# Squares of the latents summed on GpSimd, the first scale on TensorE, and the residual weighted earlier

## The chip, the cores and the metric

The kernel runs on one core of one Trainium2 chip. The core has four engines that compute: TensorE (PE in the profile, PEld for its weight loads), VectorE (DVE), ScalarE (ACT) and GpSimd (POOL). SyncE (SP) issues most of the transfers; some are issued from GpSimd's queue. Each engine works through its own queue in order. The metric is the time of one execution on the device in microseconds (us), as the median of the runs shown. The profile is one execution that was recorded in full.

## The reference

A trunk of two layers over 1024 tokens of width 1024, in float32. Each layer scales and shifts its input by values that depend on a conditioning vector c, makes one wide projection, runs three groups of attention heads on parts of it, gates, projects back, adds the residual and normalises:

```python
for l in range(DEPTH):                                   # DEPTH = 2
    mod = silu(c) @ w_ada[l] + b_ada[l]                  # adaLN
    shift, scale, gate = split(mod, 3)
    h = x * (1 + scale) + shift
    (p_cq, p_ckv, p_kr, p_qb, p_kb, p_vb, p_qc, p_kc, p_vc,
     p_qi, p_ki, p_wi, p_gate) = split(h @ w_in[l])
    cq, ckv = rms_norm(p_cq, q_norm_g[l]), rms_norm(p_ckv, kv_norm_g[l])   # the latents: 768 and 256 wide
    o_a = mla_attention(...)        # 6 heads from the latents (queries 768, keys and values 256) and rope
    o_b = dilated_attention(...)    # 6 heads, three dilation patterns, ALiBi
    o_c = sparse_attention(...)     # 4 heads; an indexer of 8 heads picks the top 256 keys of each query
    y = concat(o_a, o_b, o_c) * silu(p_gate)
    x = layer_norm(ALPHA * x + (1 + gate) * (y @ w_out[l]), ln_g[l], ln_b[l])
```

`rms_norm` needs, for each token, the mean of the squares over all features of the latent.

## The kernel before

Activations are held transposed: 8 chunks of 128 features (partitions) by 1024 tokens. TensorE multiplies in a reduced format, so every operand is kept as two tiles, a rounded high part (`hi`, by ScalarE's `Copy`) and the low rest (`lo`, by a subtraction on GpSimd or VectorE), and every product is three matmuls. `split_w` (L188) loads a raw weight tile on SP's queue and splits it; `w_chunk` fetches the weights of one chunk of 128 outputs. There are two raw tiles (`WR`) and four split ones (`W`), so two chunks are held and two more are on their way. `project` (L204) makes one chunk in two halves of 512 tokens into two PSUM banks `pj` and hands each half to a function that empties it.

The program is written in the order of the mathematics. A scheduler then sets each engine's order by running the program against its own estimate of every instruction's length: whatever is ready goes where its engine has room. So an instruction can stand in its engine's queue well ahead of, or behind, the code that it is written next to, and the order is fixed before the run. Some orders are set by tables at the top (`FB` and `FC`: how many of the latent and gate projections are used as filling work behind each head).

The stages of a layer that the change touches:

- **The start** (`begin`, L883, first layer only). For each chunk k of features `part_ada` loads two 128x1024 pieces of the adaLN weights (e = 0 for scale, e = 1 for shift), multiplies each with silu(c) in eight VectorE instructions (L913, L915) and sums over the partitions with one matmul against ones (L916); L918 adds the bias into `mod0`. `part_h` loads the chunk of x, applies scale and shift on ScalarE (L927), makes h's high part on ScalarE (L928) and its low part on GpSimd (L929; the last chunk on VectorE). `part_vb` multiplies h's chunk at once into the values of the dilated heads, accumulated for seven token blocks over seven PSUM banks (L899); the eighth block follows behind (`natural`). `LEAD` says how many chunks `part_ada` is ahead of `part_h`.
- **The indexer and the selection** (L387, L464). VectorE adds up the indexer's scores (L436), and VectorE and ScalarE search the threshold of the top 256 by bits (L462, L480). A tie-break on VectorE ends the selection (L520 to L538): a scan, and comparisons whose inputs all lie in SBUF.
- **The latents** (`latent`, L599). Eight chunks, two of ckv (i = 0, 1) and six of cq. Each half is split into `hi` and `lo`, stored to `cq_d`, squared by ScalarE (L609), transposed by TensorE in four 128x128 pieces (L614) so that tokens lie on partitions, and summed over features by VectorE (L617, L620), whose results are added up over the chunks (L621). `norm_r` makes the reciprocal roots.
- **Attention** (`attend`, L296). Scores on TensorE into three banks `S`; VectorE adds bias and takes the maximum (L283, L286, L289), ScalarE exponentiates (L291), VectorE inverts the sum (L292), GpSimd multiplies the weights by it (L293); TensorE transposes (L315, two banks `T`), the weights are split (L318, L319) and multiplied with the values (L327); the two parts of the result are added (L331, L332) and gated on GpSimd (L334).
- **The output projection** (`out_proj`, L792). For each of eight token blocks (`TBO`) TensorE makes two halves of 512 outputs, 24 matmuls each. VectorE multiplies by the gate (L856), adds the residual (L857), takes statistics (L858, L860, L862), GpSimd the reciprocal root (L863); in the last layer VectorE applies the layer norm (L867, L868) and the block is stored. The first layer stores its normalised blocks in `x1_d` without the norm's gain and offset; the second layer loads each of them as residual and GpSimd multiplies and adds them first (L843, L844). The residual's buffers `XR` are one in the first layer and two in the last.

The scratch in SBUF that GpSimd's own transfers use has the default size.

## Time and profile before

| | |
|---|---|
| runs | 1795.9 us median of 3 (1790.45 to 1797.68) |
| profiled execution | 1791.37 us, of which 1789.5 us are the recorded span |
| mean granted clock of TensorE | 0.978 |
| busy, share of the span | PE 93%, PEld 80%, DVE 78%, ACT 57%, POOL 39% |
| data moved by DMA | 178.93 MB, mean 100 GB/s |

A group row names line, engine, operation, output and inputs (buffer numbers left out), shapes and count; behind the bar stand the busy time and the mean of one in ns, and then the engine's idle time just before and what ended it. A row of the timeline begins with start and length in us; `x3` merges three instructions, and the bracket tells idle time before it and what ended it. Matmuls overlap in the pipeline, so their spacing is read from starts, not from lengths. In a stretch row stand its length and then, after the comma, the busy times of PE, PEld, DVE, ACT and POOL with their counts, TensorE's granted clock, the DMA share and GB/s. A row of slices has one digit for each 44.7 us, in tenths. A row of waits has who waited for whom, us in all, times and the longest.

### The profile page before, as it was taken

What the parts mean: (1) busy time and instruction counts of PE and PEld (TensorE: products, weight loads), DVE (VectorE), ACT (ScalarE), POOL (GpSimd) and SP (SyncE); (2) the same over time, 40 slices, a digit from 0 to 9 for tenths busy, and PEclk for the clock granted to TensorE, in tenths of its full rate; (3) what the DMA queues carried; (4) which work ended last, traced back from release to release, by engine and by line L of the source; (5) the groups of instructions that cost most, each with busy time, mean ns of one, the idle gap of its engine ahead of it and who ended that gap; (6) DMA issues with size and microseconds to landing.
All of it is one profiled execution on the core that took longest, in us unless ns stands there. A gap on an engine that the chain in (4) does not pass through costs nothing. (4 is left out here: it accounts for less than half of the span.)

```text
span 1789.5 us, 26735 instructions
## 1 busy us (share of the span) xinstructions
PE 1662.4 (93%) x9080; PEld 1440.0 (80%) x9080; DVE 1396.6 (78%) x3266; ACT 1022.0 (57%) x2010; POOL 697.8 (39%) x625
## 2 busy tenths in 40 slices
PE   4899899999998999989999989999999999998993
PEld 4778688888896888877899978888789788987882
DVE  8889788889588678886763678888948866788589
ACT  3244499895544666674113649998544367767500
POOL 3421134233434355463322113323343345666274
PEclk9899999999999999999999999999999999999997
DMA  9465113233212521222332212242220244122232
GB/s 345 147 220 189 48 55 92 78 119 102 75 36 62 212 92 57 84 68 92 110 130 51 71 59 56 75 142 83 74 92 20 67 171 141 45 76 91 71 106 94
DMA packets 55364, 178.93 MB, mean 100 GB/s; under 512 B 7606, under 2 KB 8630, under 8 KB 54716
## 3 DMA queue, kind: packets, MB, share of 16 engines
q1 hardware_dynamic: 50812, 147.86, 24.7%
q0 software_dynamic: 4416, 29.36, 5.7%
q8 instruction: 72, 1.18, 0.3%
q14 instruction: 64, 0.52, 0.1%
HBM read 129.74 MB, written 34.87 MB: 92 GB/s over the span
## 5 line engine op out<-in xcount | busy, mean ns | idle before, releaser
L199 PE MATMUL pj<-h,w 128*128 128x512 f32 (+1 forms) x3408 | 831.1, 391 | 13.9 <-DVE qk L233 5.4
L199 PEld LDWEIGHTS pj<-h,w 128*128 128x128 f32 x3408 | 632.2, 191 | 131.6 <-issue 12.6
L193 POOL TENSOR_TENSOR w<-wr,w 128x1024 fp32r<-128x1024 f32 (+2 forms) x86 | 192.9, 2244 | 284.4 <-ACT w L192 262.7
L199 PE MATMUL S<-qk,qk 128*128 128x512 f32 (+2 forms) x1104 | 281.9, 360 | 11.0 <-DVE mx L283 4.6
L293 POOL TENSOR_SCALAR pr<-pr,den 128x896 f32<-128x896 f32 (+7 forms) x180 | 139.0, 776 | 257.3 <-DVE den L292 214.0
L318 ACT ACTIVATE pt<-T 128x512 fp32r<-128x512 f32 (+1 forms) x320 | 172.1, 551 | 112.6 <-PE T L315 56.3
L319 DVE TENSOR_TENSOR pt<-T,pt 128x512 fp32r<-128x512 f32 (+1 forms) x320 | 199.6, 633 | 43.1 <-ACT pt L318 38.9
L327 PE MATMUL O<-pt,v 128*128 128x256 f32 (+1 forms) x1280 | 213.0, 286 | 7.3 <-DVE pt L319 4.2
L199 PEld LDWEIGHTS S<-qk,qk 128*128 128x128 f32 x1104 | 185.2, 191 | 36.7 <-DVE mx L283 8.7
L480 ACT ACTIVATE scr<-acc,U 128x768 uint8<-128x768 f32 x186 | 193.2, 1039 | 33.6 <-DVE U L476 18.1
L327 PEld LDWEIGHTS O<-pt,v 128*128 128x128 f32 x1280 | 185.6, 191 | 24.0 <-DVE pt L319 6.8
L334 POOL TENSOR_TENSOR g<-g,osum 64x256 f32<-64x256 f32 x128 | 98.6, 770 | 224.0 <-DVE osum L332 222.3
L291 ACT ACTIVATE pr<-pr,mx 128x384 f32<-128x384 f32 (+7 forms) x188 | 145.6, 775 | 54.7 <-DVE mx L283 36.4
L315 PE MATMUL T<-ident,pr 128*128 128x128 f32 x852 | 144.7, 278 | 9.7 <-POOL pr L293 5.1
L462 DVE TENSOR_SCALAR_CACHE_REDUCE scr<-acc,U 128x384 uint8<-128x384 f32 x186 | 138.4, 744 | 3.8
L192 ACT ACTIVATE w<-wr 128x1024 fp32r<-128x1024 f32 (+2 forms) x86 | 83.8, 976 | 65.0 <-PE pj L199 62.3
L315 PEld LDWEIGHTS T<-ident,pr 128*128 128x128 f32 x852 | 101.4, 141 | 21.0 <-POOL pr L293 6.5
L199 PE MATMUL pj<-w,h 128*128 128x256 f32 (+2 forms) x672 | 107.0, 300 | 1.4 <-DMA h<-cq_d 1.2
L199 PEld LDWEIGHTS pj<-w,h 128*128 128x128 f32 x672 | 91.7, 190 | 6.3 <-DMA h<-cq_d 1.4
L331 ACT ACTIVATE osum<-O 64x256 f32<-64x256 f32 x128 | 48.6, 380 | 58.5 <-PE O L327 55.3
L436 DVE SCALAR_TENSOR_TENSOR acc<-S,wi,acc 128x512 f32<-128x512 f32 (+1 forms) x84 | 56.2, 679 | 30.6 <-ACT S L431 30.3
L332 DVE TENSOR_TENSOR osum<-O,osum 64x256 f32<-64x256 f32 x128 | 53.4, 417 | 26.2 <-ACT osum L331 22.6
(277 smaller groups left out, 2565.2 us busy)
## 6 DMA issues: line engine op xcount, KB each, us to landing
wr<-in_wt_dram SPq DMA_DIRECT2D x62, 512.0 KB, 3.6
cq_d<-rw SPq DMA_DIRECT2D x64, 256.0 KB, 2.0
h<-cq_d POOLq DMA_DIRECT2D x4, 4096.0 KB, 20.2
qk<-qk POOLq DMA_DIRECT2D x48, 256.0 KB, 2.9
pt<-in_w_ada_dram SPq DMA_DIRECT2D x22, 512.0 KB, 4.0
wr<-in_w_out_dram SPq DMA_DIRECT2D x16, 512.0 KB, 3.5
bi<-in_bias_dram SPq DMA_DIRECT2D x14, 512.0 KB, 4.1
bi<-in_w_ada_dram SPq DMA_DIRECT2D x10, 512.0 KB, 4.5
```

The costliest lines, as they stand in the source:

```text
L192: act.activation(hi[:, :n], raw[:, :n], AF.Copy)
L193: (lo_eng or pool).tensor_tensor(lo[:, :n], raw[:, :n], bc(hi[:, :n]), OP.subtract)
L199: pe.matmul(ps, lhsT=l, rhs=r, start=(i == 0), stop=(i == len(items) - 1))
L291: act.activation(p[:, :n], p[:, :n], AF.Exp, bias=m, scale=-1.0, accum_out=den)
L293: (dve if ne[qb] else pool).tensor_scalar(p[:, :n], p[:, :n], den, 0.5, OP.mult, OP.mult)
L315: pe.transpose(t[:, c:c + P], p[j](2 * kp + kk), ident)
L318: act.activation(pt[:, 0, :n], t[:, :n], AF.Copy)
L319: dve.tensor_tensor(pt[:, 1, :n], t[:, :n], bc(pt[:, 0, :n]), OP.subtract)
L327: pe.matmul(o[:, oc], lhsT=vt(kb), rhs=pt[:, e, pc], start=(kb == 0 and e == 0), stop=(kb == 2 * g + 1 and e == 1), skip_group_check=True)
L334: pool.tensor_tensor(yc, yc, s[r0:r0 + 64], OP.mult)
L462: dve.tensor_scalar(scr8[:, :IDX_LEN[b]], scores(b), s, None, op, OP.add, accum_out=dst[:, b:b + 1])
L480: act.activation(scr[:, :IDX_LEN[b]], scores(b), AF.Sign, bias=U[:, b:b + 1].bitcast(F32), accum_out=cnt[:, b:b + 1])
```

## The change

- **Latents.** Two tiles (`RES` for ckv, `LNG` for cq) hold the squares of the first chunk; GpSimd adds the squares of each later chunk to them (24 additions of 128x512 over both layers). Only after the last chunk of each latent are four transposes for each half made, and one reduction: 32 transposes in place of 128, and 8 reductions in place of 32.
- **Start.** The scale (e = 0) is made on TensorE: eight accumulating matmuls with the weight piece as stationary operand and a column of silu(c) as the moving one, in place of eight VectorE instructions and one matmul. The shift stays as it was. The low parts of h and of the value weights are made on VectorE in place of GpSimd. `LEAD` is 1, and `part_h` stands ahead of `part_ada`.
- **Residual.** In the second layer the weighting by gain and offset of the first layer's norm is emitted behind the latent heads 0 to 3, two blocks each (`NRES`): load into `RES`, multiply and add on GpSimd, store to `xw_d`. The output projection loads the weighted block from there, and has `RES` as one more residual buffer in both layers. `LNG` and `LNB` hold the gain and offset; the last layer's are loaded into the same tiles after that.
- The three new tiles (12 KB a partition) are paid for by a smaller scratch for GpSimd's transfers.

```diff
-LEAD = 3
+LEAD = 1
+NRES = ((0,0,0,0,0,0),(2,2,2,2,0,0))
...
+    RES, LNG, LNB = [sb.tile([P, 1024], F32, name=n) for n in ("res", "lng", "lnb")]
+    xw_d = [dr.tile([P, 1024], F32, name=f"xw_d{i}") for i in range(NB)]
...
     def latent(l, i):
-        sums = rk if i < 2 else scq
+        sums, row = (rk, RES) if i < 2 else (scq, LNG)
...
-            hi, lo, sq = RW.next().bitcast(F32R), RW.next().bitcast(F32R), PR.next()
+            hi, lo = RW.next().bitcast(F32R), RW.next().bitcast(F32R)
+            sq = row[:, cols] if i in (0, 2) else PR.next()
...
             act.activation(sq, ps, AF.Square)
...
-            t = ps_t.tile([P, 4, P], F32, name="T")
-            for j in range(4):
-                pe.transpose(t[:, j, :], sq[:, j * P:(j + 1) * P], ident)
-            to = sums[:, half * 4:half * 4 + 4]
-            if i in (0, 2):
-                dve.tensor_reduce(to, t, AX.X, OP.add)
-            else:
-                s4 = small.tile([P, 4], F32, name="s4")
-                dve.tensor_reduce(s4, t, AX.X, OP.add)
-                dve.tensor_tensor(to, to, s4, OP.add)
+            if i not in (0, 2):
+                pool.tensor_tensor(row[:, cols], row[:, cols], sq, OP.add)
+            if i in (1, 7):
+                t = ps_t.tile([P, 4, P], F32, name="T")
+                for j in range(4):
+                    pe.transpose(t[:, j, :], row[:, cols.start + j * P:cols.start + j * P + P], ident)
+                dve.tensor_reduce(sums[:, half * 4:half * 4 + 4], t, AX.X, OP.add)
...
     def mla(l, values):
...
+            for _ in range(NRES[l][h]):
+                residual(rest.pop(0))
+
+    def residual(i):
+
+        if i == 0:
+            sp.dma_start(LNG, a["ln_g"][0].to_broadcast([P, 1024]))
+            sp.dma_start(LNB, a["ln_b"][0].to_broadcast([P, 1024]))
+        tb = TBO[i]
+        sp.dma_start(RES, x1_d[tb])
+        pool.tensor_tensor(RES, RES, LNG, OP.mult)
+        pool.tensor_tensor(RES, RES, LNB, OP.add)
+        sp.dma_start(xw_d[tb], RES)
...
     def out_proj(l):
-        XR = Ring([AC[0]] + ([G.tiles[f]] if last else []))
+        XR = Ring([AC[0], RES] + ([G.tiles[f]] if last else []))
...
-            sp.dma_start(xr, x1_d[tb] if last else a["x"][tb])
-            if last:
-                pool.tensor_tensor(xr, xr, lgb[0], OP.mult)
-                pool.tensor_tensor(xr, xr, lgb[1], OP.add)
+            sp.dma_start(xr, xw_d[tb] if last else a["x"][tb])
...
         def part_ada(k):
...
+                to = o_ps[:, 0, 2 * k + e:2 * k + e + 1]
+                if e == 0:
+                    for c in range(8):
+                        pe.matmul(to, lhsT=w[:, c * P:(c + 1) * P], rhs=cs[:, c:c + 1], start=(c == 0), stop=(c == 7),
+                                  skip_group_check=True)
+                    continue
...
         def part_h(k):
-                hi, lo = split_w(a["wvb"][0, k // 2], 784, ring=QK, raws=raws)
+                hi, lo = split_w(a["wvb"][0, k // 2], 784, ring=QK, lo_eng=dve, raws=raws)
...
-            (dve if k == 7 else pool).tensor_tensor(HA[k][1], x, bc(HA[k][0]), OP.subtract)
+            dve.tensor_tensor(HA[k][1], x, bc(HA[k][0]), OP.subtract)
...
-    nc = bacc.Bacc("TRN2", target_bir_lowering=False, num_devices=1)
+    nc = bacc.Bacc("TRN2", target_bir_lowering=False, num_devices=1, dynamic_dma_scratch_size=4096)
```

The scheduler's order at the three places that matter most. A row has the line in its own file, so the same statement has another number in the changed kernel (L193 is L198 there, L293 is L298, L334 is L339, L617 is L625, L233 is L238).

GpSimd's queue at the program's start, before; `qk` are the value weights' parts, `h` the chunks of h, `w` the weight chunks of the indexer:

```order
L193 TENSOR_TENSOR qk_77<-wr_91,qk_76 128x784
L929 TENSOR_TENSOR h<-v,h 128x1024 x2
L193 TENSOR_TENSOR qk_79<-wr_92,qk_78 128x784
L929 TENSOR_TENSOR h<-v,h 128x1024 x2
L193 TENSOR_TENSOR qk_81<-pt_89,qk_80 128x784
L193 TENSOR_TENSOR qk_83<-pt_90,qk_82 128x784
L929 TENSOR_TENSOR h<-v,h 128x1024 x2
L193 TENSOR_TENSOR w_85<-wr_91,w_84 128x1024
L929 TENSOR_TENSOR h<-v,h 128x1024
L193 TENSOR_TENSOR w_87<-wr_92,w_86 128x1024
```

And now, with the indexer's first instructions behind them:

```order
L198 TENSOR_TENSOR w_85<-wr_91,w_84 128x1024
L198 TENSOR_TENSOR w_87<-wr_92,w_86 128x1024
L410 TENSOR_TENSOR rw_100<-rw_100,pr_93 32x512
L198 TENSOR_TENSOR w_85<-wr_91,w_84 128x1024
L241 DMA qk_76<-qk_76 64x1024
L242 DMA qk_77<-qk_77 64x1024
```

The eleven subtractions of the start have left this queue (for VectorE's); two weight splits stay.

GpSimd's queue in the second layer, in the sparse heads, where VectorE does the selection's tie-break, before:

```order
L334 TENSOR_TENSOR g_8696<-g_8696,osum 64x256
L193 TENSOR_TENSOR w_87<-wr_92,w_86 128x1024
L193 TENSOR_TENSOR w_85<-wr_91,w_84 128x1024
L293 TENSOR_SCALAR bi_8693<-bi_8693,den 128x256
L334 TENSOR_TENSOR g_8696<-g_8696,osum 64x256
L193 TENSOR_TENSOR w_87<-wr_92,w_86 128x1024
L236 DMA qk_80<-qk_80 64x1024
```

And now (`res` is the residual, weighted by `lng` and `lnb`):

```order
L805 TENSOR_TENSOR res<-res,lng 128x1024
L339 TENSOR_TENSOR g_8615<-g_8615,osum 64x256
L806 TENSOR_TENSOR res<-res,lnb 128x1024
L198 TENSOR_TENSOR w_87<-wr_92,w_86 128x1024
L198 TENSOR_TENSOR w_85<-wr_91,w_84 128x1024
L805 TENSOR_TENSOR res<-res,lng 128x1024
L339 TENSOR_TENSOR g_8615<-g_8615,osum 64x256
L806 TENSOR_TENSOR res<-res,lnb 128x1024
L198 TENSOR_TENSOR w_87<-wr_92,w_86 128x1024
L805 TENSOR_TENSOR res<-res,lng 128x1024
L241 DMA qk_80<-qk_80 64x1024
```

The residual's instructions, written behind the latent heads, stand here one whole group of heads earlier, between the splits of the weights. All sixteen stand from just behind the last latent to the end of the tie-break.

VectorE's queue in the first layer where the indexer ends, the first two latents are summed and the first dilated head's projection is emptied from the banks `pj`, before:

```order
L226 TENSOR_TENSOR qk_76<-pj,qk_76 64x512
L441 TENSOR_TENSOR acc<-acc,causb 128x128
L436 SCALAR_TENSOR_TENSOR acc<-S,wi,acc 128x512
L617 TENSOR_REDUCE rk<-T 128x4
L462 TENSOR_SCALAR scr,cnt_124<-acc 128x512
L226 TENSOR_TENSOR qk_76<-pj,qk_76 64x512
L436 SCALAR_TENSOR_TENSOR acc<-S,wi,acc 128x512
L441 TENSOR_TENSOR acc<-acc,causb 128x128
L617 TENSOR_REDUCE rk<-T 128x4
L233 TENSOR_TENSOR qk_78<-pj,qk_77 64x512
L462 TENSOR_SCALAR scr,cnt_124<-acc 128x640
L620 TENSOR_REDUCE s_1548<-T 128x4
```

And now:

```order
L231 TENSOR_TENSOR qk_76<-pj,qk_76 64x512
L446 TENSOR_TENSOR acc<-acc,causb 128x128
L441 SCALAR_TENSOR_TENSOR acc<-S,wi,acc 128x512
L625 TENSOR_REDUCE rk<-T 128x4
L467 TENSOR_SCALAR scr,cnt_127<-acc 128x512
L231 TENSOR_TENSOR qk_76<-pj,qk_76 64x512
L441 SCALAR_TENSOR_TENSOR acc<-S,wi,acc 128x512
L446 TENSOR_TENSOR acc<-acc,causb 128x128
L625 TENSOR_REDUCE rk<-T 128x4
L238 TENSOR_TENSOR qk_78<-pj,qk_77 64x512
L467 TENSOR_SCALAR scr,cnt_127<-acc 128x640
L238 TENSOR_TENSOR qk_78<-pj,qk_77 64x512
```

Ahead of the first instruction that empties the second part of a bank (L233, now L238) stand as many instructions as before, two reductions among them; only the reductions behind it are gone.

More of the change, by code (lines that the diff above doesn't have):

```diff
@@ L758, in query @@
             project(wh, wl, 6, CA, evac)
-        q, y = {}, {}
+        q, y, rest = {}, {}, list(range(NB))
         keys(0)
@@ L821, in out_proj @@
         sp.dma_start(g1, g1_d[l].to_broadcast([P, 1024]))
-        lgb = []
         if last:
-            for t, src in zip([fresh("pt0", F32), fresh("pt1", F32), PR3[2], PR3[1]],
-                              (a["ln_g"][0], a["ln_b"][0], a["ln_g"][1], a["ln_b"][1])):
-                sp.dma_start(t, src.to_broadcast([P, 1024]))
-                lgb.append(t)
+            sp.dma_start(LNG, a["ln_g"][l].to_broadcast([P, 1024]))
+            sp.dma_start(LNB, a["ln_b"][l].to_broadcast([P, 1024]))
         else:
@@ L866, in out_proj @@
                     cols = slice(n * 512, (n + 1) * 512)
-                    dve.scalar_tensor_tensor(r[:, cols], r[:, cols], mv[:, 0:1], lgb[2][:, cols], OP.subtract, OP.mult)
-                    dve.scalar_tensor_tensor(r[:, cols], r[:, cols], rs, lgb[3][:, cols], OP.mult, OP.add)
+                    dve.scalar_tensor_tensor(r[:, cols], r[:, cols], mv[:, 0:1], LNG[:, cols], OP.subtract, OP.mult)
+                    dve.scalar_tensor_tensor(r[:, cols], r[:, cols], rs, LNB[:, cols], OP.mult, OP.add)
                     sp.dma_start(out[tb][:, cols], r[:, cols])
@@ L908, in part_ada @@
                     dve.tensor_scalar(bcol[:, 0, :], bcol[:, 0, :], 1.0, None, OP.add)
-                part = cols[:, (2 * k + e) % 8, :]
+                to = o_ps[:, 0, 2 * k + e:2 * k + e + 1]
[4 more added lines that the diff above has]
+                    continue
+                part = cols[:, k % 8, :]
                 for c in range(8):
@@ L915, in part_ada @@
                         dve.scalar_tensor_tensor(part, wc, cs[:, c:c + 1], part, OP.mult, OP.add)
-                pe.matmul(o_ps[:, 0, 2 * k + e:2 * k + e + 1], lhsT=part, rhs=ones, start=True, stop=True,
-                          skip_group_check=True)
+                pe.matmul(to, lhsT=part, rhs=ones, start=True, stop=True, skip_group_check=True)
             dve.tensor_tensor(mod0[:, :, k], o_ps[:, 0, 2 * k:2 * k + 2], bcol[:, :, k], OP.add)
@@ L928, in part_h @@
             act.activation(HA[k][0], x, AF.Copy)
-            (dve if k == 7 else pool).tensor_tensor(HA[k][1], x, bc(HA[k][0]), OP.subtract)
+            dve.tensor_tensor(HA[k][1], x, bc(HA[k][0]), OP.subtract)
         for k in range(-LEAD, 9):
+            if 0 <= k < 8:
+                part_h(k)
             if 0 <= k + LEAD < 8:
                 part_ada(k + LEAD)
-            if 0 <= k < 8:
-                part_h(k)
             if k > 0:
```

## The prediction, made before the changed kernel was run

> **What bounds the kernel now.** I read the page's busy times and slices first, then the stretches at both ends, then the timeline at the places that the change touches.
>
> ```profile
> span 1789.5 us, 26735 instructions
> PE 1662.4 (93%) x9080; PEld 1440.0 (80%) x9080; DVE 1396.6 (78%) x3266; ACT 1022.0 (57%) x2010; POOL 697.8 (39%) x625
> PE   4899899999998999989999989999999999998993
> 1760.00:1789.50 29.50, 0.60 (x3) 0.18 (x1) 25.76 (x39) 0.00 (x0) 9.44 (x7) 0.57 0.27 98
> ```
>
> TensorE is the bound through the middle: its slices read 8 or 9. It falls off in the first two slices and in the last, where in 29.5 us it works 0.60 (first number) while VectorE works 25.76 (third). So time is to be had from work on TensorE in the middle and from whatever holds TensorE or the output up at the two ends. GpSimd has 61% of the span free.
>
> **The end.** In the second layer's output projection GpSimd weights each residual block (L843, L844) while VectorE finishes blocks. The rows show one such meeting, TensorE's last matmul, the distance of two blocks on TensorE, and the last block's finish, which nothing disturbs.
>
> ```profile
> L843 POOL TENSOR_TENSOR acc<-acc,pt 128x1024 f32<-128x1024 f32 x4 | 10.7, 2680 | 8.2 <-DMA acc<-x_d 8.1 <-DMA pt<-in_ln_g_dram 0.2
> 1730.68 1.52 PE L199 MATMUL pj<-v,h 128*128 128x512 f32 x6
> 1741.56 1.52 PE L199 MATMUL pj<-v,h 128*128 128x512 f32 x6
> 1754.87 1.66 PE L199 MATMUL pj<-v,h 128*128 128x512 f32 x6 [2.26 <-DVE acc L856]
> 1755.11 2.56 POOL L843 TENSOR_TENSOR acc<-acc,pt 128x1024 f32<-128x1024 f32 x1 [2.34 <-DMA acc<-x_d]
> 1755.45 5.58 DVE L868 SCALAR_TENSOR_TENSOR pr<-pr,rs,pr 128x512 f32<-128x512 f32 x2
> 1760.21 0.39 PE L199 MATMUL pj<-rw,h 128*128 128x512 f32 x1
> ...
> 1780.72 0.69 DVE L856 TENSOR_TENSOR pr<-pj,bi 128x512 f32<-128x512 f32 x1
> ...
> 1784.53 1.41 DVE L868 SCALAR_TENSOR_TENSOR pr<-pr,rs,pr 128x512 f32<-128x512 f32 x2
> ```
>
> Two instructions of L868 take 5.58 us beside GpSimd and 1.41 without: VectorE stands while GpSimd runs a two-input instruction. L856, which reads one input from PSUM, is not stretched. TensorE needs 1741.56 - 1730.68 = 10.9 us a block. VectorE alone needs three instructions of 512 columns for the first half of a block (L856 and two more, 0.69 each), then 1780.72 to 1785.94 for the second half and the finish: 2.1 + 5.2 = 7.3 us. So VectorE is late only through the sixteen GpSimd instructions (16 x 2.65 = 42 us), and ends 28.9 us behind the last matmul (1760.6 to 1789.5). The change moves the sixteen away and loads finished blocks; the earlier loads are into three buffers and not late. Then only the last block's finish follows the last matmul: 1780.72 to 1789.5, 8.8 us. Gain 28.9 - 8.8 = 20.1, and the wait of 2.26 before 1754.87 with it: **22.4 us**. Ends: 15 if VectorE still trails by one block of 7.3; not more than 22.4.
>
> **The start.** The h of chunk k needs scale and shift from the adaLN weights (16 loads), made by 128 VectorE instructions, then two of ScalarE and a subtraction on GpSimd.
>
> ```profile
> 24.36 2.44 POOL L929 TENSOR_TENSOR h<-v,h 128x1024 fp32r<-128x1024 f32 x1 [1.18 <-ACT h L928]
> 24.50 2.45 DVE L915 SCALAR_TENSOR_TENSOR g<-pr,cs,g 128x128 f32<-128x128 f32 x1
> 31.83 0.61 PE L916 MATMUL O<-ones,g 128*128 128x1 f32 x4
> 42.14 0.70 PE L899 MATMUL S<-qk,h 128*128 128x392 f32 x3
> 42.28 1.23 ACT L927 ACTIVATE v<-v,mod 128x1024 f32<-128x1024 f32 x1
> 42.67 0.52 PE L899 MATMUL T<-qk,h 128*128 128x392 f32 x2
> 44.16 1.04 ACT L928 ACTIVATE h<-v 128x1024 fp32r<-128x1024 f32 x1
> 54.27 1.18 PE L899 MATMUL S<-qk,h 128*128 128x392 f32 x3
> 55.25 0.86 PE L899 MATMUL T<-qk,h 128*128 128x392 f32 x2
> 78.70 14.24 PE L199 MATMUL pj<-h,w 128*128 128x512 f32 x66
> ...
> 10.00:20.00 10.00, 1.76 (x6) 1.50 (x6) 10.00 (x39) 3.04 (x3) 1.01 (x1) 1.00 1.03 415
> 50.00:60.00 10.00, 6.98 (x28) 6.98 (x29) 9.89 (x28) 3.24 (x3) 6.95 (x3) 0.66 0.10 35
> ```
>
> The last two rows are stretches: VectorE is full (10.00, 9.89), and at 50 to 60 the queues are nearly idle (35 GB/s against 415), so VectorE is the bound there, not the loads. One VectorE instruction of 128x128, 0.34 us by itself, takes 2.45 beside GpSimd. The change takes 64 of the 128 off VectorE; puts 64 matmuls of one column on TensorE, at most 0.61 / 4 = 0.15 each, 9.8 us less the 1.2 of eight that go; and moves the seven subtractions and four weight splits from GpSimd to VectorE, where a 1024-wide one costs about 1.4 (twice L856's 0.69). VectorE then has about 8 x (8 x 0.34 + 1.4) + 4 = 37 us of work where it is now full past 60. The next limits are two. The loads before the last x, about 16 MB at 415 GB/s, are in near 42; the chain behind (1.4 for the scale, 2.3 on ScalarE, 21 matmuls at 0.53 / 3 = 0.18, 24 more for the eighth block) ends at 54. TensorE: first h near 14.5 (loads by 10, a split on ScalarE and VectorE, 2.3 on ScalarE), then 168 x 0.18 = 30, 6/8 of the one-column matmuls 8, the 24 of the eighth block 4.3, about 2 for a slow clock at first (0.33 a matmul at 54.27, against 0.18), 2.6 where chunk 1's shift stands behind chunk 0's matmuls, 2 from the two weight splits that GpSimd keeps: 63.4. The chunk projection that starts at 78.70 starts there: **15 us**, taken between 24 (the loads' end) and 2 (rival below). LEAD 1 shortens the queue of loads ahead of x; it is in these numbers.
>
> **The latents.** Of 128 transposes of squares, 96 go. In the middle of the layer and at the start of selection they look like this:
>
> ```profile
> 403.45 0.60 PE L614 MATMUL T<-ident,pr 128*128 128x128 f32 x4
> 403.81 5.75 PE L199 MATMUL pj<-h,w 128*128 128x512 f32 x24
> ...
> 214.91 0.69 DVE L233 TENSOR_TENSOR qk<-pj,qk 64x512 fp32r<-64x512 f32 x1
> 215.70 10.49 PE L199 MATMUL pj<-h,w 128*128 128x512 f32 x40
> ...
> L620 DVE TENSOR_REDUCE s<-T 128x4 f32<-128x512 f32 x24 | 16.2, 687 | 0.2
> L372 POOL TENSOR_TENSOR h<-g,h 128x512 fp32r<-128x512 f32 x8 | 10.9, 1367 | 34.2 <-ACT h L371 34.2
> ```
>
> Four occupy TensorE from 403.45 to 403.81, 0.09 each. 80 of the 96 stand in such full stretches: 80 x 0.09 = **7.2 us** (0 to 8). The other 16 stand, eight a layer, where TensorE waits anyway: its next projection needs the PSUM bank that L233 empties at 215.6 and starts at 215.70. VectorE's row there keeps as many instructions ahead of that L233, so I count nothing. 24 reductions of 0.69 leave VectorE, at nothing gained, since TensorE is full beside them. 24 additions of 128x512 enter GpSimd, about 1.37 each by L372, 33 us, on an engine that is busy 39% of the time; the sources of the next VectorE instructions are in PSUM, as L856's, so nothing is blocked: 0, at most 10 where an addition stands ahead of a softmax weight. [...]
>
> **The residual, moved.** Emitted in the second layer's attention, its GpSimd instructions stand, in that queue's row, earlier: from the last latents through the dilated heads' end, six of the sixteen among the top-k's tie-break. There VectorE has two-input work from SBUF:
>
> ```profile
> 1382.21 5.29 POOL L193 TENSOR_TENSOR w<-wr,w 128x1024 fp32r<-128x1024 f32 x2 [6.00 <-ACT w L192]
> 1382.48 2.82 DVE L538 SCALAR_TENSOR_TENSOR acc<-scr,bi 128x640 f32<-128x640 uint8 x1
> 1385.56 2.37 DVE L527 TENSOR_SCALAR scr<-acc,thr 128x768 uint8<-128x768 f32 x1
> 1385.69 0.62 PE L199 MATMUL S<-qk,qk 128*128 128x384 f32 x2 [0.70 <-DVE mx L283]
> 1388.40 12.32 PE L199 MATMUL pj<-h,w 128*128 128x512 f32 x46 [2.09 <-DVE v L359]
> 1393.49 0.96 DVE L538 SCALAR_TENSOR_TENSOR acc<-scr,bi 128x768 f32<-128x768 uint8 x1
> 1394.48 0.69 DVE L527 TENSOR_SCALAR scr<-acc,thr 128x896 uint8<-128x896 f32 x1
> PE T L315 <- POOL pr L293: 5.1, 5, 2.0
> wr<-in_wt_dram SPq DMA_DIRECT2D x62, 512.0 KB, 3.6
> ```
>
> Beside L193, L538 takes 2.82 for 0.96 and L527 2.37 for 0.69: 1.8 us a GpSimd instruction, and TensorE waited 0.70 + 2.09 = 2.8 of these 3.6. Six times 1.8 x 0.78 is **8 us lost**. The other ten precede softmax weights (L293), for which TensorE waits 5.1 us in the whole run; I add nothing. Ends: 0 and 30. Sixteen DMAs are added on SP's queue; each store waits for GpSimd, and weight loads stand behind it. Two raw tiles and two split ones put the weights two chunks ahead, and a chunk is 48 matmuls (twice 5.75 us at 403.81): 23 us against a round of 12.5 (below), so I cost that at nothing. The second x buffer in the first layer's output projection: nothing, TensorE is full there.
>
> **Sum.** 1789.5 - 22.4 - 15 - 7.2 + 8 = 1752.9 us of span. The profiled execution took 1791.4, 1.9 more, and the median of three, 1795.9, is 4.5 above it: 1759 us. One per cent of this kernel is 18 us; 0.5%, 9 us, is what a measurement can tell.
>
> **Rivals.**
> - The start hardly gains. At 54.27 the matmuls run at 0.33 instead of 0.18 after a gap. If each of seven chunks leaves TensorE a gap and its first twelve matmuls run so, 12 x 0.15 = 1.8 us is lost on each, 13 in all, and 2 are left of 15: 1772. For it: ScalarE's 2.3 us lie between scale and matmul. Against: in the new order scales of the next chunks mostly stand ahead of a chunk's matmuls. [...]
> - The residual takes back more in the tie-break, 15 to 30 us instead of 8: 1766 to 1781. For it: VectorE there is what TensorE waits for, and reordered attention follows.
> - The end does not empty: VectorE or a late load still holds it, gain 5: 1776. Against: 7.3 us of work a block against 10.9.
> - Slower: the single residual buffer. A load (3.6), two GpSimd instructions (5.3) and a store, taken as long as a load, are a round of 12.5 us, and a GpSimd that waits for the load blocks every softmax weight behind it. It decides from (36.6 + 8 + 9) / 8 = 6.7 us a residual passed on to TensorE; at 8 us each, 1759 - 8 + 64 = 1815. Against: the order leaves two or three instructions between rounds, and TensorE hardly waits for GpSimd now.
>
> **Chances.** Forecast, 1746 to 1772: 0.64; start 0.12; tie-break 0.14; end 0.06; slower 0.04. Range 1742 to 1783: below, the start at its best; above, the tie-break's and the end's cases. Faster than 1787: 0.92; within 0.5%: 0.04 (a poor end and a dear tie-break together); slower: 0.04.
>
> **What would show it.** End: last output about 9 us behind the last matmul, no VectorE instruction above 1.5 us per pair there. Start: the first chunk projection of 48 and more matmuls near 63. Latents: 32 transposes of squares, no gain around the early ones. Residual: VectorE's tie-break instructions above 2 us, more than now, and TensorE idle in 1330 to 1400. I am wrong if TensorE's idle time in the middle grows by over 20 us, or if the last matmul comes no earlier than 1745.

## The result, and the profile after

The changed kernel took 1766.5 us (median of 4 runs, 1765.2 to 1771.7) against 1796.7 (1790.5 to 1797.7): 0.9845 of the time before, interval 0.9815 to 0.9874, 30 us faster. The forecast was 1759 (1742 to 1783), 37 us faster. Timed again on another occasion it came to 0.9868 (0.9844 to 0.9892). So sign and range held. The forecast was a ratio of 0.9794 (1759 to 1795.9); by the two ratios measured, 9 to 13 us of the gain did not come. The page of its profile, with the rows that were read first of the kernel before:

```profile
span 1769.9 us, 26708 instructions
PE 1670.7 (94%) x9096; PEld 1449.3 (82%) x9096; DVE 1344.7 (76%) x3165; ACT 1020.3 (58%) x2010; POOL 696.9 (39%) x638
PE   8999899999998999989999999999999799998998
```

Both ends of TensorE's row are filled now. In the middle a 7 has appeared, at 1372 to 1416 us, where a 9 stood. This profiled execution took 1771.7, the slowest of its four runs, and that of before was one of the fastest of its own: the spans differ by 19.6 us, the medians by 30.

**The end.** The last stretch of the span, TensorE's last matmul, and VectorE's first and last instruction for the last block:

```profile
1761.00:1769.87 8.87, 0.45 (x2) 0.02 (x1) 5.09 (x9) 0.00 (x0) 0.92 (x1) 0.68 0.16 59
1761.06 0.39 PE L204 MATMUL pj<-rw,h 128*128 128x512 f32 x1
1761.48 0.69 DVE L867 TENSOR_TENSOR pr<-pj,bi 128x512 f32<-128x512 f32 x1 [3.29 <-PE pj L204]
1765.30 1.41 DVE L879 SCALAR_TENSOR_TENSOR pr<-pr,rs,lnb 128x512 f32<-128x512 f32 x2
```

The output ends 8.4 us behind the last matmul (1761.45 to 1769.87) instead of 28.9, and VectorE does only nine instructions in it. But the last matmul stands at 1761, where it stood before (1760.6): whatever was won ahead of it was lost again in this execution.

**The start.** Two stretches of 10 us, a group of sixteen of the new one-column matmuls (L924) at each speed, three matmuls at each speed, and the first chunk projection:

```profile
20.00:30.00 10.00, 9.74 (x48) 9.66 (x47) 6.42 (x15) 5.46 (x5) 0.00 (x0) 0.67 1.02 406
30.00:40.00 10.00, 10.00 (x46) 10.00 (x45) 6.07 (x15) 3.05 (x3) 0.00 (x0) 0.65 1.04 386
21.83 2.15 PE L924 MATMUL O<-cs,bi 128*128 128x1 f32 x16 [0.26 <-DVE mod L936]
25.06 1.18 PE L910 MATMUL S<-qk,h 128*128 128x392 f32 x3
28.98 3.41 PE L924 MATMUL O<-cs,g 128*128 128x1 f32 x16
38.85 0.70 PE L910 MATMUL S<-qk,h 128*128 128x392 f32 x3
39.74 1.84 PE L924 MATMUL O<-cs,pr 128*128 128x1 f32 x16
71.79 14.24 PE L204 MATMUL pj<-h,w 128*128 128x512 f32 x66
```

TensorE is full (9.74, 10.00) and VectorE is not (6.42, 6.07): the bound has moved. The granted clock is 0.67 and 0.65; from 23.4 to 37.1 us, 13.65 us in all, it is 0.50 (called half clock from here on). The projection starts at 71.8 instead of 78.7, not at 63.4.

**The tie-break of the second layer.** First its stretch from the first scan to its end in the kernel before:

```profile
1363.58:1417.33 53.75, 49.30 (x293) 43.22 (x292) 52.30 (x79) 17.20 (x33) 19.23 (x13) 0.97 0.17 50
```

Then the changed kernel: the stretch from its last counts to its first scan and the one from there to its end, GpSimd's root of the latents' sum, the residual's first instruction, its first in the tie-break and its last, two VectorE instructions of the tie-break, and TensorE's longest wait:

```profile
1279.53:1347.79 68.26, 65.45 (x382) 57.01 (x381) 39.57 (x110) 30.54 (x64) 45.76 (x35) 1.00 0.39 132
1347.79:1411.48 63.69, 50.26 (x285) 42.86 (x283) 62.43 (x70) 14.83 (x27) 35.19 (x18) 0.92 0.37 122
1292.46 1.68 POOL L646 TENSOR_TENSOR scq<-scq,mhalf 128x8 f32<-128x8 f32 x1
1296.63 2.40 POOL L805 TENSOR_TENSOR res<-res,lng 128x1024 f32<-128x1024 f32 x1 [2.49 <-DMA lng<-in_ln_g_dram]
1351.77 2.39 POOL L805 TENSOR_TENSOR res<-res,lng 128x1024 f32<-128x1024 f32 x1 [3.97 <-DMA res<-x_d]
1376.77 2.62 DVE L532 TENSOR_SCALAR scr<-acc,thr 128x768 uint8<-128x768 f32 x1
1384.95 3.03 DVE L543 SCALAR_TENSOR_TENSOR acc<-scr,bi 128x768 f32<-128x768 uint8 x1
1394.10 7.99 PE L204 MATMUL pj<-h,w 128*128 128x512 f32 x24 [5.91 <-DVE qk L238]
1404.95 2.68 POOL L806 TENSOR_TENSOR res<-res,lnb 128x1024 f32<-128x1024 f32 x1
```

From 1351.77 to the end eight of the residual's sixteen instructions run in the tie-break; the other eight run just ahead of it, from 1296.63. L532 takes 2.62 us for 768 columns, where 896 columns take 0.69 undisturbed, and L543 takes 3.03 for 768 columns, which take 0.96 undisturbed. VectorE is full (62.43 of 63.69). TensorE stands for 13.4 us, where it stood for 4.45 before, and for 2.8 in the stretch ahead: 16.2 in all. The bracket at 1296.63 names what held the residual back until then: the load of the gain into `LNG`, the tile in which the latents' squares were summed until just before.

### The profile page after: what moved, and what is told of

It reads as the page before. It is cut to its first block, busy times and chain, and to the rows that moved or that the text cites. A ratio compares the mean times of both kernels' runs of the same rounds, so it can differ in the third digit from the quotient of the medians.

```text
span 1769.9 us, 26708 instructions
## 1 busy us (share of the span) xinstructions
PE 1670.7 (94%) x9096; PEld 1449.3 (82%) x9096; DVE 1344.7 (76%) x3165; ACT 1020.3 (58%) x2010; POOL 696.9 (39%) x638
## 4 chain that ended last, share of the span: by engine, by line
PE 59%; DVE 21%; ACT 10%; issue 5%; DMA 4%; POOL 1%; SPq 0%; DVEq 0%; ACTq 0%; POOLq 0%
PE pj L204 33%; PE S L204 12%; PE O L332 5%; ACT scr L485 4%; PE T L320 4%; DVE pt L324 2%; DVE scr L467 2%; DVE pr L536 1%; DVE acc L441 1%; ACT pr L296 1%; ACT pt L323 1%; DVE acc L543 1%; DVE g L261 1%; DVE pr L288 1%; PE T L204 1%
## 5 line engine op out<-in xcount | busy, mean ns | idle before, releaser
L198 POOL TENSOR_TENSOR w<-wr,w 128x1024 fp32r<-128x1024 f32 (+2 forms) x86 | 190.7, 2218 | 301.0 <-ACT w L197 290.4
L204 PE MATMUL S<-qk,qk 128*128 128x384 f32 (+2 forms) x1104 | 279.2, 361 | 15.0 <-DVE mx L288 8.4
L204 PEld LDWEIGHTS S<-qk,qk 128*128 128x128 f32 x1104 | 187.6, 192 | 41.8 <-DVE mx L288 10.2
L298 POOL TENSOR_SCALAR pr<-pr,den 128x640 f32<-128x640 f32 (+7 forms) x182 | 138.9, 767 | 205.2 <-DVE den L297 164.9
L296 ACT ACTIVATE pr<-pr,mx 128x128 f32<-128x128 f32 (+7 forms) x192 | 146.4, 763 | 51.0 <-DVE mx L288 35.7
L339 POOL TENSOR_TENSOR g<-g,osum 64x256 f32<-64x256 f32 x128 | 98.9, 773 | 191.7 <-DVE osum L337 179.0
L320 PEld LDWEIGHTS T<-ident,pr 128*128 128x128 f32 x849 | 100.5, 141 | 19.2 <-issue 6.0
```

The costliest lines, as they stand in the source:

```text
L198: (lo_eng or pool).tensor_tensor(lo[:, :n], raw[:, :n], bc(hi[:, :n]), OP.subtract)
L204: pe.matmul(ps, lhsT=l, rhs=r, start=(i == 0), stop=(i == len(items) - 1))
L296: act.activation(p[:, :n], p[:, :n], AF.Exp, bias=m, scale=-1.0, accum_out=den)
L298: (dve if ne[qb] else pool).tensor_scalar(p[:, :n], p[:, :n], den, 0.5, OP.mult, OP.mult)
L320: pe.transpose(t[:, c:c + P], p[j](2 * kp + kk), ident)
L339: pool.tensor_tensor(yc, yc, s[r0:r0 + 64], OP.mult)
```

## The experiments

Ratios are to the kernel before, on the same chip and the same occasion; compare them, not microseconds of different occasions. Where the expectations speak of 52.9, 14.8 or 16.6 us in the tie-break, its stretch is taken from the last counts (1279.53 us in the changed kernel), with all sixteen of the residual's instructions inside; from its first scan on there are eight.

| kernel | median us | ratio | interval |
|---|---|---|---|
| changed | 1766.5; again 1769.2 | 0.9845; 0.9868 | 0.9815 to 0.9874; 0.9844 to 0.9892 |
| latents' part alone | 1790.1 | 0.9979 | 0.9963 to 0.9995 |
| start's part alone | 1784.8 | 0.9951 | 0.9934 to 0.9968 |
| residual's part alone | 1762.7 | 0.9830 | 0.9808 to 0.9853 |
| changed, nothing weighted | 1748.7 | 0.9753 | 0.9727 to 0.9778 |
| changed, residual first | 1754.6 | 0.9791 | 0.9771 to 0.9812 |
| the same, scale half on TensorE | 1747.5 | 0.9754 | 0.9734 to 0.9773 |
| the same, scale on VectorE | 1768.7 | 0.9877 | 0.9854 to 0.9899 |
| the same, scale 128 wide | 1750.8 | 0.9775 | 0.9752 to 0.9799 |
| changed without latents' part | 1751.8 | 0.9777 | 0.9755 to 0.9799 |
| residual first, half and wide | 1752.3 | 0.9777 | 0.9754 to 0.9799 |
| no latents, half and wide | 1758.0 | 0.9811 | 0.9789 to 0.9832 |

The three parts alone sum to 0.0021 + 0.0049 + 0.0170 = 0.0240, that is 43 us, and the residual alone is at least as good as the whole change. The whole is worth 0.0132 to 0.0155: 15 to 19 us are lost where the parts meet. The changed kernel was timed on two of the four occasions, the second time together with the last three kernels of the table. Its ratio differs by 0.0023 (4 us) between the two, so differences from it across occasions are good to some 4 us.

**The latents' part alone** (`latent`'s part of the diff, the new tiles and the smaller scratch).

> The kernel before with the latents' part alone. Forecast's theory: 80 of the 96 transposes that go stand in full stretches of TensorE, 0.09 us each, so 7 us faster than before, 1789 to 1790, and nothing at the early latents. Rival: the new order of the middle gives it back (TensorE's idle time behind 100 us grew from 63.4 to 79.6 us between the two profiles), and the part alone is worth nothing: 1797, within 3 us of before.

4 us faster: between the two. The first layer's tie-break from its first scan, in the kernel before and then in this one, and the wait behind it in this one:

```profile
507.88:562.75 54.87, 49.70 (x287) 43.01 (x286) 53.20 (x84) 18.27 (x36) 20.33 (x13) 0.97 0.16 49
```

```profile
511.47:563.62 52.15, 42.31 (x251) 37.00 (x249) 50.53 (x69) 15.38 (x27) 17.67 (x10) 0.95 0.17 52
564.72 3.02 PE L201 MATMUL S<-qk,qk 128*128 128x512 f32 x8 [6.56 <-DVE mx L285]
```

TensorE is idle for 9.8 us there instead of 5.2. The transposes that went stood nowhere near (the last at 416 us before the change). But the scheduler made another order: VectorE now does 69 instructions in the stretch instead of 84, the last seven of the tie-break in one piece, and the attention that TensorE waits for stands behind them. At the early latents nothing was gained, as forecast: the projection that starts at 215.70 before starts at 220.50 here. This profiled execution has the span of the one before (1789.3 and 1789.5 us); the 4 us are those of the medians.

**The start's part alone** (`begin` and `LEAD`).

> The kernel before with the start's part alone. Forecast: the first chunk projection 15 us earlier, near 63, and 15 us faster, 1782. What the changed kernel's profile says: the projection starts at 71.8 instead of 78.7, 6.9 us, and TensorE has no free time left before it (the one-column matmuls are two records each and hold it some 20 us, a part of it at half clock); then 7 us faster at most, 1790, and 4 us (1793) if the 3 us that are lost again before 210 belong to this part.

9 us faster, more than the 7 read from the changed kernel's profile and less than the 15 forecast. Its projection starts at 73.3 in the profile, 5.4 us earlier, with 17.1 us at half clock on the way, the most of the six profiles that have this start; that execution took 1787.9, three more than the median.

**The residual's part alone** (`residual`, `out_proj`, the new tiles).

> The kernel before with the residual's part alone. Forecast: 22.4 us off the end, 8 back in the tie-break of the second layer, 1782. Read from the changed kernel's profile: 20 off the end, 10 back (TensorE's gaps in the tie-break 14.8 us instead of 4.5), 1786 to 1787. Rival: the tie-break and what follows take all of it, 1797.

30 us faster: all three expectations were wrong, and too low. GpSimd's first and last instruction of the residual, and the second layer's tie-break from its first scan:

```profile
915.04 2.39 POOL L806 TENSOR_TENSOR res<-res,lng 128x1024 f32<-128x1024 f32 x1 [2.33 <-DMA res<-x_d]
999.80 2.41 POOL L807 TENSOR_TENSOR res<-res,lnb 128x1024 f32<-128x1024 f32 x1
1358.93:1412.67 53.74, 49.30 (x293) 43.26 (x292) 52.29 (x79) 17.20 (x33) 19.22 (x13) 0.97 0.17 50
```

Without the latents' part nothing else uses `RES` and `LNG`, and the scheduler puts the sixteen, though they are written behind the latent heads, at 915 to 1002 us, into the indexer. The tie-break is as it was before the change: 53.7 us, TensorE idle for 4.4 (53.75 and 4.45 before).

**Nothing weighted.** `mla` doesn't call `residual`, and the output projection loads `x1_d`; so gain and offset of the first layer are left out of the residual.

> The changed kernel without the weighting of the residual in the second layer's attention (the output projection adds the first layer's block without gain and offset): sixteen GpSimd instructions and sixteen transfers less in the middle, all else the same. If the GpSimd instructions in the tie-break cost 10 us, it is 10 us faster than the changed kernel, 1756, VectorE's tie-break instructions sum to about 43 us instead of 52.9, and TensorE's gaps there fall from 14.8 to about 4.5. If the order of the middle costs it, whatever GpSimd does there, it stays within 3 us of 1766 and the gaps stay.

0.9753: the gain is 16 to 21 us over the changed kernel, more than expected. VectorE's tie-break instructions sum to 40.2 us, and TensorE's gaps in the stretch for which 14.8 and 16.6 are quoted are 7.8. Its profile also has the better start (67, see below), so not all of the difference is the residual's.

**The residual written first.**

```diff
-            for _ in range(NRES[l][h]):
-                residual(rest.pop(0))
...
+        for i in range(NB if l else 0):
+            residual(i)
         jobs = [lambda i=i: latent(l, i) for i in range(8)] + ...
```

> The whole change, with the residual's weighting written ahead of the second layer's latents instead of behind the latent heads. The latents' squares use the same two tiles (RES and LNG), so in the changed kernel the weighting cannot start before the last latent is summed, and then it falls into the tie-break; in the kernel with the residual's part alone it ran at 915 to 1003 us, in the indexer. If that is what the change loses, this one is 17 to 18 us faster than the changed kernel, 1749, as without any weighting (1748.7), with the sixteen instructions near 900 to 1000, the tie-break's sum at 40 to 42 us instead of 52.9 and TensorE's gaps there at 4 to 8 us instead of 16.6. Rival: GpSimd's two-input instructions cost VectorE as much wherever they stand, and it stays within 5 us of 1766.

```profile
912.05 2.38 POOL L803 TENSOR_TENSOR res<-res,lng 128x1024 f32<-128x1024 f32 x1 [2.49 <-DMA res<-x_d]
1277.82:1341.57 63.75, 63.75 (x376) 56.35 (x374) 38.82 (x111) 31.57 (x66) 27.09 (x27) 1.00 0.26 83
1341.57:1391.73 50.16, 42.31 (x273) 38.33 (x272) 48.55 (x69) 13.61 (x25) 12.63 (x9) 0.93 0.15 48
```

Place and tie-break are as expected: the two stretches that in the changed kernel took 68.3 and 63.7 us, with 2.8 and 13.4 of idle on TensorE, take 63.8 and 50.2, with none and 7.85. VectorE's tie-break instructions sum to 40.2 us for 52.9, 12.7 less, which is about 1.6 us for each of the eight GpSimd instructions that lay among them. The time is 0.9791, 10 to 14 us better than the changed kernel's 0.9845 and 0.9868. Against the second of these the rival's 5 us lie outside the interval (8 to 20), against the first they do not (3 to 16); the tie-break's own stretches settle it, with 18 us less in them. Of the 17 expected, some are missing in the median. The same sixteen instructions cost 10 to 14 us more in and ahead of the tie-break than in the indexer.

**Scale half on TensorE** (from the residual-first kernel).

```diff
-                if e == 0:
+                if e == 0 and k % 2 == 0:
...
-                part = cols[:, k % 8, :]
+                part = cols[:, (2 * k + e) % 8, :]
```

> The kernel just above, with the scale on TensorE for the even chunks only and on VectorE for the odd ones. In the changed kernel's start TensorE is what is full (gaps of 3.2 us before the chunk projection at 71.8, one-column matmuls 22.0 us) and VectorE works 51.8 of 71.8 us. If that is the bound, 9 us leave TensorE and 11 enter VectorE, both stay under 63, the projection starts near 64 to 66 and the kernel is 5 to 7 us faster than the one above. Rival: VectorE becomes the bound again, as before (80.1 of 78.7 us), and nothing is gained: within 2 us of the one above.

7 us faster in the medians, as expected, but not in the way expected: the projection starts at 69.95 instead of 71.20, and another 4 us come between there and 250 us. Why was not followed further. (The 51.8 and 80.1 us of the expectation seem to add up instructions' lengths, which overlap; the stretches give VectorE 45.79 of 71.79 us in the changed kernel and 67.86 of 78.70 before.) It has the lowest ratio of the kernels that compute everything, and its interval (0.9734 to 0.9773) lies below both of the changed kernel's, though it overlaps those of others around 0.9775.

**Scale wholly on VectorE** (`if e == 0` never taken, `part` as just above).

> The residual-first kernel with the scale wholly on VectorE as before the change; the low parts on VectorE, LEAD and the order of the start as changed. If VectorE was slow in the start only through the lock by GpSimd's subtractions, 128 instructions of 0.34 us and 14 us of low parts are 57 us, the projection starts at 64 to 70 and the total is that of the residual-first kernel within 3 us or a little better: the first scale on TensorE bought nothing. Rival: the move to TensorE is what gains, and without it the projection starts near 77, 5 to 6 us slower than the residual-first kernel.

The rival. A stretch of its start, one of TensorE's waits, and the projection:

```profile
30.00:40.00 10.00, 8.73 (x50) 8.37 (x50) 10.00 (x30) 3.89 (x4) 2.14 (x1) 1.00 1.01 389
24.89 1.02 PE L908 MATMUL pj<-qk,h 128*128 128x392 f32 x2 [2.71 <-ACT h L944]
76.60 9.06 PE L204 MATMUL pj<-h,w 128*128 128x512 f32 x39
```

VectorE is full (10.00; 9.84 and 9.93 in the stretches beside this one) with GpSimd nearly idle, TensorE waits at the head of chunks, and the projection starts 5.4 us later. The 57 us for VectorE were too few. Of the other 9 us of the 14 by which it is slower, most are lost between 250 and 800 us, where TensorE is idle for 31.3 us against 24.7 in the residual-first kernel. The two kernels do the same work there, in another order; which instruction of it costs the time was not followed.

**Scale 128 columns wide.**

```diff
-                    pe.matmul(to, lhsT=w[:, c * P:(c + 1) * P], rhs=cs[:, c:c + 1], ...
+                    pe.matmul(o_ps[:, 0, x:x + P], lhsT=w[:, c * P:(c + 1) * P],
+                              rhs=cs[:, c:c + 1].to_broadcast([P, P]), ...
```

> The residual-first kernel with the scale's matmuls 128 columns wide (the same column repeated) instead of one; a record of 128x128 takes 0.11 us like one of a single column at full clock, so the work is the same. The changed kernel's clock was 0.5 from 23.3 to 36.9 us, right behind a group of sixteen one-column records, though TensorE's gaps there are 0.3 us. If the clock follows the columns that stream and not the time that TensorE is busy, that stretch shrinks to a third or goes, and the projection starts 4 to 7 us earlier than 71.8, near 66. If it follows busy time or comes by chance, the stretch stays and the total is within 3 us of the residual-first kernel.

```profile
15.03 0.60 PE L908 MATMUL pj<-qk,h 128*128 128x392 f32 x2
20.00:30.00 10.00, 9.20 (x64) 9.12 (x64) 8.11 (x19) 5.45 (x6) 0.00 (x0) 1.00 1.02 406
30.00:40.00 10.00, 9.55 (x68) 9.38 (x67) 8.03 (x19) 5.42 (x6) 0.00 (x0) 1.00 1.04 385
66.14 14.24 PE L204 MATMUL pj<-h,w 128*128 128x512 f32 x66
```

No half clock after the first rise, and that rise at 15 us instead of 19 to 20: the projection starts 5.1 us earlier. The median is 3.8 us lower, and the intervals overlap (0.9752 to 0.9799 and 0.9771 to 0.9812), so the start is shown to be shorter in its profile, and the whole kernel is not shown to be faster.

**The changed kernel again.**

> The changed kernel itself, to time it on the same chip as the three below and to have a second profile of its start. Its time stays at 0.981 to 0.988 of the kernel before. If the clock's stretch at half speed in the start hangs on where a fixed grid of 3.4 us falls against the one-column groups (13.7 us of it with the first clock event at 20.0, 19.9 and 19.5 us, 3.4 us with it at 19.2), it has about 13.7 us again when the first event lies at 19.5 to 20.1, less when it lies elsewhere; the chunk projection then starts near 72 or near 67.

```profile
20.00:30.00 10.00, 9.55 (x68) 9.38 (x67) 7.93 (x20) 5.98 (x6) 0.00 (x0) 1.00 1.02 408
30.00:40.00 10.00, 10.00 (x70) 10.00 (x68) 7.61 (x17) 5.90 (x6) 0.88 (x1) 1.00 1.04 381
66.70 14.24 PE L204 MATMUL pj<-h,w 128*128 128x512 f32 x66
```

The same program, with the clock whole in these stretches: first rise (from which on the 392-column matmuls are 0.18 us apart) at 18.95 us, 3.4 us at half clock afterwards, projection at 66.7. This execution took 1759.9 us and was the fastest of six; the other five took 1766.3 to 1771.8. Of the 11.9 us between the two spans (1769.9 and 1758.0) 10 are there by 200 us. Its tie-break is as in the first profile (eight of the residual's inside, 63.5 us), so what was said of that doesn't hang on one execution.

**Without the latents' part.**

> The start's and the residual's part without the latents' part (squares transposed chunk by chunk as before, no shared tiles). The parts alone were worth 0.0049 and 0.0170 of the time, 0.978 together if they add up; then the residual runs in the indexer again, unasked, and the time is 1751 to 1755 against 1795 before, 10 to 14 us better than the changed kernel: the latents' part costs the change what its tiles' sharing forces, and brings at most the 4 us that it was worth alone. Rival: the loss of the changed kernel is in the middle's new order, which the start's part brings as well, and this one stays within 5 us of it.

```profile
903.16 2.38 POOL L807 TENSOR_TENSOR res<-res,lng 128x1024 f32<-128x1024 f32 x1 [2.06 <-DMA res<-x_d]
100.00:250.00 150.00, 142.43 (x692) 118.54 (x691) 134.56 (x265) 92.74 (x183) 33.25 (x24) 0.98 0.35 113
250.00:850.00 600.00, 576.58 (x3303) 498.69 (x3302) 474.94 (x1216) 386.79 (x778) 256.33 (x252) 0.99 0.28 93
```

The place is as expected, with the residual in the indexer unasked, and the gain is a little more than the 10 to 14 us expected: 17 us by the medians, 16 by the ratios, against the changed kernel on the same occasion. The two parts add up (0.9777 for 0.978). For comparison, the first two stretches with the latents' part, in the residual-first kernel:

```profile
100.00:250.00 150.00, 140.18 (x671) 117.44 (x671) 128.85 (x245) 89.47 (x178) 32.88 (x24) 0.95 0.37 118
250.00:850.00 600.00, 572.63 (x3265) 495.70 (x3264) 468.22 (x1204) 392.40 (x788) 268.22 (x260) 0.99 0.29 92
```

With the latents' part TensorE stands for 9.8 + 27.4 us in the two, without it for 7.6 + 23.4: of the 48 transposes saved in this layer (0.09 us each at 403.45 in the kernel before) nothing is left. In the whole the latents' part was worth nothing that these two can tell (0.9791 with it, 0.9777 without, intervals overlapping, on two occasions).

**Half and wide together, with and without the latents' part.**

> Residual first, the scale on TensorE for the even chunks only, and those matmuls 128 columns wide. The half alone was 0.9754 of before with 13.7 us at half clock in the start, the width alone 0.9775 with none. If both add: no or 3.4 us at half clock, projection at 62 to 66, 0.971 to 0.974. If the half leaves gaps on TensorE that cool it anyway (10.3 us of gaps in the half's start), 0.975 as with the half alone.

> As the one above, but without the latents' part and with the residual written where the change puts it. If the latents' part is worth its 4 us in the whole, this one is 4 us slower than the one above; if the middle's order decides, it is equal or faster by up to 5 us.

They don't add: 0.9777 for 0.9754 and 0.9775 alone. The half's start leaves TensorE gaps (10.6 us up to the projection at 67.4, 10.2 us at half clock). Without the latents' part it is 6 us slower, where equal or faster was the rival and 4 slower the first expectation. Most of that looks like the start again: the projection comes at 71.75 there, 4.3 us later, behind 14.2 us of gaps. So this pair doesn't show a worth of the latents' part either.

## Why the prediction was right, and where it was wrong

**The end: right.** 28.9 us became 8.4 (8.8 said), the wait of 2.26 went, and no pair of VectorE's takes over 1.41 there. That is 22.7 us for 22.4. The cause, GpSimd's two-input instructions standing in VectorE's way, shows on the other side too: moved into the tie-break they stretch VectorE's instructions there (3.03 us for 0.96) as they did at the end (5.58 for 1.41). L856, which reads one input from PSUM, took 0.67 to 0.69 us all sixteen times in the second layer of the kernel before, also where L843 ran beside it (0.68 at 1745.34, L843 from 1744.83 for 2.85).

**The start: mechanism right, size wrong.** 15 us said; 6.9 in one profile, 12.0 in the other. VectorE was indeed freed, and TensorE became the next limit as said. Two terms of TensorE's sum were mis-sized. The first: sixty-four one-column matmuls at 0.15 us, 9.8 in all, 8 of them behind the first h. Each of them is two records (rows that the profiler writes for one matmul), as the row `O<-cs,bi x16` for eight matmuls shows; one record takes at most 0.115 us at full clock (1.84 / 16) and 0.21 at half (3.41 / 16). With the sixteen of the shift they hold TensorE for 22.0 us (20.2 in the second profile), some 14 of them behind the first h (13 in the second) where 8 were said. The row that I priced them by, L916 x4 in 0.61, was itself two matmuls of two records. The second: 2 us for a slow clock. The matmuls of 392 columns took 41.3 instead of the 34.4 that 192 take at 0.179, 7 us more (4 in the second profile). The first h came at 15.4 instead of 14.5. On the other side the 2.6 and 2 us set down for waits did not come: behind the first h TensorE has 0.7 us of gaps, and 2.5 ahead of it. The rival on the clock (13 us lost to gaps) came in part, and for another cause: from the first h on 18.3 us ran at half clock in the first profile, some 9 us lost, and 7.3 in the second, some 4 (half of each stretch, an estimate from the 0.50), with none of the gaps that it needs.

**The latents: the wrong step is that 80 of the 96 stand in full stretches and so their whole time is gained.** TensorE was full where the transposes stood, but the order behind them is not kept when they go. Alone 4 us of the 7.2 came; 4.6 us of new idle time in the first layer's tie-break would cover the rest, though the order changed elsewhere too. In the whole nothing came that could be told from noise. That the sixteen early ones gain nothing was right.

**The residual: right in place and price, a little short.** Six instructions in the tie-break at 1.8 us of VectorE were said; eight at about 1.6 were measured. (The 1.8 set each stretched instruction against an undisturbed one of the next larger size.) That the other ten, which precede softmax weights, cost nothing was short: ahead of the tie-break TensorE has 2.8 us of idle that the residual-first kernel has not. 10 to 14 us were lost where 8 were said. What the prediction did not see is that the residual need not have stood there at all: the same diff sums the squares in the residual's tiles and so bars the way into the indexer. The order had the fact in plain sight, "from the last latents".

**The sum.** For the two profiles of the changed kernel, against 1789.5: end -22.7 and -22.8, start -6.9 and -12.0, the middle +10.0 and +3.3 (what is left to 1769.9 and 1758.0), where -7.2 + 8 = +0.8 was said. So the error is the start and the middle (the latents' 7 and the residual's excess), in about equal shares. I had written that I would be wrong if the last matmul came no earlier than 1745: it came at 1761 and 1750. By that test the sum ahead of the end was wrong, and the total stayed in the range because the end, the largest term, was exact. The other sign did not come: from 100 to 1740 us TensorE's idle time grew from 61.2 to 79.6 us and to 73.7 in the second profile, by less than 20. Part of the nearness is luck. I had added 6.4 us from the span to the median; here the profiled execution was the slowest, and the median lies 3.4 below its span. So the span missed the sum's 1752.9 by 17 us and the median missed 1759 by 7.5.

## What to carry to other kernels

When one change reuses another's buffers, look at the tile's previous user: it sets the earliest start of the new work, and the scheduler put that work where it first could, here into the one place where it hurts; writing it ahead of the other user won 10 to 14 us. Price a new matmul by records, not by statements, and at both speeds measured (0.115 and 0.21 us for a one-column record here). A part that saves work on a full engine may not be worth the time it saves, if the scheduler makes a new order behind it; measure the parts alone and together.

## What the runs showed of the hardware

In the changed kernel the clock fell to 0.50 at 23.4 us, though TensorE had stood for only 0.3 us since 15.4: the group at 21.83 is sixteen weight loads with one column each. In the profile of the wide form, with 128 columns behind the same loads, it reads 1.00 in both stretches from 20 to 40 us, and it rose at 15 us instead of 19 to 20. The changes of the clock that the traces record, 28 in the kernel before and 30 in the changed one, go only between 0.50 and 1.00, and in each trace they lie whole steps of 3.413 us apart (13.65 is four of them).

What went ahead of the first rise, in the same two profiles: in the changed kernel TensorE was busy with one-column matmuls from 11.93 us (sixteen, 3.57 us), and the matmuls of 392 columns behind them, from 15.36 on, stayed 0.33 us apart until 20.0. In the wide form it was busy with 128 columns from 11.69 (sixteen, 3.59 us), and the matmuls of 392 columns from 15.03 on are 0.18 us apart. That it is the columns is not shown by these two alone. There is one profile of the wholly wide form. Of the two with every other chunk wide, one rose at 8.96 us, right behind its first wide group, fell again at 12.4 in a gap of 4.3 us, and rose again at 19.2; the other rose at 20.3 and then did not fall before 54.4. That the clock did not fall at 23 us in the wholly wide form could still be chance, as in three profiles of the narrow one; that it rose 4 to 5 us earlier is in none of the six.

How long the half clock lasted went with the time of the first rise. Six profiles have this start on TensorE (the changed kernel twice, the start alone, nothing weighted, residual first, no latents): where the clock first rose at 18.75, 18.95 and 19.17 us, 3.4 us at half clock followed before the projection, which started at 66.2 to 66.7; at 19.49, 19.89 and 20.02 us, 13.7 to 17.1 followed, and it started at 71.2 to 73.3. It is the likely cause of the spread of the changed kernel's runs from 1760 to 1772; only two of them were profiled. One trap in reading it, in the changed kernel again:

```profile
10.00:20.00 10.00, 8.27 (x31) 8.19 (x32) 7.77 (x20) 3.95 (x4) 0.00 (x0) 1.00 1.03 417
16.16 1.18 PE L910 MATMUL S<-qk,h 128*128 128x392 f32 x3
```

The stretch reads a granted clock of 1.00, yet the three matmuls are 0.33 us apart, as at half. The clock column holds only recorded changes, and none was recorded before 20 us; ahead of the first, the speed is to be read from the distance of the matmuls.
